# A mixture-of-experts tail on one core: the first top-16 inside the score stage, separate rings for weights and gathered rows

## The chip, the cores and the metric

The kernel runs on one core of a Trainium2 chip. The metric is the device time of one execution in microseconds (us). TensorE (PE) multiplies matrices, VectorE (DVE) and ScalarE (ACT) do elementwise work, GpSimd (POOL) does elementwise work and issues indirect transfers, and SyncE (SP) issues the other transfers. Each engine takes its instructions in the order in which the program lists them; semaphores order them across engines.

## What is computed

Two transformer blocks run over 512 tokens of 1024 features. The change touches only the last part, the `peer` layer of the second block, whose input `h` has been normalised. Cut to that:

```python
def peer(h, w_pq, sub_keys, expert_u, expert_v):          # 8 heads, 2 halves, 128 keys a half
    def one(xb):
        q = (xb @ w_pq).reshape(PEER_BLOCK, PEER_HEADS, 2, PEER_DKH)
        s = jnp.einsum('thpd,hpkd->thpk', q, sub_keys).astype(jnp.float32)
        sv, si = lax.top_k(s, PEER_TOPK)                   # the first top-16: 16 key sets
        cand = (sv[:, :, 0, :, None] + sv[:, :, 1, None, :]).reshape(PEER_BLOCK, PEER_HEADS, -1)
        cidx = (si[:, :, 0, :, None] * N_KEYS + si[:, :, 1, None, :]).reshape(PEER_BLOCK, PEER_HEADS, -1)
        best, pos = lax.top_k(cand, PEER_TOPK)             # the second top-16, for each head
        eidx = jnp.take_along_axis(cidx, pos, axis=-1)
        g = jax.nn.softmax(best, axis=-1)
        act = jax.nn.gelu(jnp.einsum('thkd,td->thk', expert_u[eidx], xb).astype(jnp.float32), approximate=False)
        return jnp.einsum('thk,thkd->td', (g * act).astype(xb.dtype), expert_v[eidx])
```

There are 128 x 128 experts, each with a row of 1024 numbers in `expert_u` and one in `expert_v`, and every token uses 8 x 16 = 128 of them.

## The kernel before, in words

A matrix product is made of three matmuls with operands that are split in a high and a low part (`mm3`, lines 124 to 126). `wload` (L109) brings in a block of weights: SP loads 512 KB into a place of the ring `raw` (L106), ACT rounds it to the high part `whi` (L117), and DVE, or POOL where the caller says so, subtracts to get the low part `wlo` (L118), which frees the place in the ring. Activations are split in the same way by `split` (L152, L153).

`peer` (L1565) has three stages.

1. **Score stage** (`scores`, L1646). For each of 16 key sets (8 heads x 2 halves) a block of `w_pq` is loaded and multiplied with `h` (24 matmuls), and `keys` (L1650) multiplies the result with that set's keys (4 matmuls, L1653), copies the 4 x 128 x 128 scores to `psc` (L1655) and stores them in DRAM as `scd` (L1656). The keys `sk` are loaded once as a whole. The `w_pq` loads have their low part on DVE.
2. **Route** (`route`, L1687). For each of four tiles t of 128 tokens: load that tile's scores from `scd` (L1693); 16 first top-16 (`top16`, L1678: two MAX8, two FIND_INDEX8, one MATCH_REPLACE8, here over 128 scores); turn the indices into `sf` (L1701); form 50 candidates for each head (L1708) and take 8 second top-16; find the chosen experts (`pick`, L1784) and the gates. For t = 0 the route ends there with a list of expert numbers, because the first 128 tokens fetch their rows. For the other 384 tokens, 32 batches of one-hot matrices (`oj` L1765, `oi` L1767, L1773) for each tile give, through 4 matmuls a batch (L1775), a dense table of gates, in which each of 128 blocks of 128 experts has one gate for each token and expert; the table goes to `stage` (L1777), and two thirds of it to DRAM (`gd`, L1782). `route` is a generator: at each `yield n, engine` the caller computes `n` blocks of `up` (L1795), with the low part of the weights on that engine. An `up` loads block i of `u` transposed (`uT`), multiplies with `h` of the 384 tokens (24 matmuls 128x384) and applies Gelu (L1802); in this stage the result goes to DRAM (`actd`). The first NPRE = 60 blocks are made here, 20 with the low part on POOL and 40 on DVE.
3. **Tail**, 128 blocks (the loop in `peer`). `mixed` (L1807) gets block i's activations, from `actd` if i < 60, else by an `up` here, multiplies them with the gates (`gt` loaded for two blocks at a time; the products go to a tile `ew`, L1822, L1824) and splits the product; `down` (L1830) loads block i of `v` and runs 18 matmuls of 128x512, which add to six accumulators. `mixed` runs AHEAD = 2 blocks ahead of `down`. For the first 128 tokens `gathered` (L1838) takes 256 rows, one for each partition at a time: 128 of `u` (product with `h`, L1856), then 128 of `v` (multiply-add into the output, L1869). POOL issues each row's indirect transfer (L1848), LAG = 2 rows ahead of their use. One row is taken per block while i < 60, and 196 over the 66 blocks from 60 to 125. In words of this text, the blocks below 60 are *early* ones and the others *mixed* ones. `wload`'s blocks and the gathered rows share the ring `raw` of RING = 6 places of 512 KB. After block 127 the results are scaled and added to the residual (L1616 to L1633).

The order on each engine is set when the program is built, by a scheduler that simulates the engines and picks among instructions whose inputs and buffers it holds to be ready; the places of rings and pools enter into it, so a change of a ring also changes the order.

Of the kernel before, what the change touches and what calls it, by code (L numbers as in the profile page):

```python
# [7 lines left out]
F32 = mybir.dt.float32  # L8
F32R = mybir.dt.float32r
I32 = mybir.dt.int32  # L10
U32 = mybir.dt.uint32
# [4 lines left out]
P = 128  # L16
D = 1024
# [10 lines left out]
class Kern:  # L28
# [1536 lines left out]
    def peer(self, h, first, residual, done):  # L1565

        nc, a = self.nc, self.a
        mod = self.mod2
        hhi, hlo = h
        with ExitStack() as c:  # L1570
            p0 = self.pool(c, "pe0")
            h0 = self.h0 = self.t(p0, [P, D], "h0")
            with ExitStack() as c1:
                qp = self.pool(c1, "pq")
                self.sk = self.t(qp, [P, 16, P], "sk")
                nc.sync.dma_start(self.sk, a["sk"])
                self.scores(qp, hhi, hlo, first, residual)
                done()
            pp = self.pool(c, "pe")
            self.stage = self.t(pp, [P, 2, P, 64], "stage")  # L1580
            with ExitStack() as c2:
                rp = self.pool(c2, "pr")
                self.iota16 = self.t(rp, [P, 16], "iota")
                nc.sync.dma_start(self.iota16, a["iota16"])
                self.iota = self.t(rp, [P, P], "iota128")
                nc.sync.dma_start(self.iota, a["iota128"])
                self.row0 = self.t(rp, [P, 16], "row0")
                nc.sync.dma_start(self.row0, a["row0"])
                jobs = self.route(rp, pp)
                pre = 0  # L1590
                for n, eng in jobs:
                    for _ in range(n):
                        if pre < self.NPRE:
                            self.up(pp, pre, hhi, hlo, eng)
                            pre += 1
            while pre < self.NPRE:
                self.up(pp, pre, hhi, hlo)
# [25 lines left out]
            for t in range(4):  # L1623
                for i in range(2):
                    s = slice(512 * i, 512 * i + 512)
# [3 lines left out]
                    else:  # L1629
                        z = self.raw()[:, :512]  # L1630
# [1 line left out]
                        (nc.vector if 2 * t + i > 4 else nc.gpsimd).tensor_add(xt[t][:, s], xt[t][:, s], z)  # L1632
                    nc.sync.dma_start(a["out"][t * P : t * P + P, s], xt[t][:, s])  # L1633

    NPRE = 60
    PROD = 5
    BOUND = (6, 14), (3, 8)
    BOUND2 = (6, 14), (8, 17)
    BOUND3 = (6, 12), (2, 8)
    RING = 6  # L1640
    AHEAD = 2
    EARLY = 2
    LAG = 2
    WB = 3

    def scores(self, p, hhi, hlo, first, residual):  # L1646

        nc, a = self.nc, self.a

        def keys(m, q):  # L1650
            pk = self.mm_ps()
            for t in range(4):
                nc.tensor.matmul(pk[:, t * P : t * P + P], q[:, t * P : t * P + P], self.sk[:, m], start=True, stop=True)  # L1653
            s = self.t(p, [P, 4, P], "psc", bufs=2)
            nc.scalar.copy(s, pk.rearrange("p (t k) -> p t k", t=4))  # L1655
            nc.sync.dma_start(a["scd"].rearrange("t p m k -> p t m k")[:, :, m], s)  # L1656

        h = list(zip(hhi, hlo))
        qs = [self.t(p, [P, S], "pq", bufs=3) for _ in first]
        self.halves(first, h, lambda n, ps, cs: nc.scalar.copy(qs[n][:, cs], ps[:, cs]), lambda i: None)  # L1660
        last = list(enumerate(qs))
        norm = self.last_hi, self.last_split
        for m in range(len(first), 16):
            with self.after(*norm):
                w = self.cut(*self.wload(a["w_pq"][m]))
            ps = self.mm_ps()
            self.proj_feat(w, h, ps)
            for z in last:
                keys(*z)
            q = self.t(p, [P, S], "pq", bufs=3)  # L1670
            nc.scalar.copy(q, ps)
            last = [(m, q)]
            if 4 <= m < 12:
                with self.after(*norm):
                    residual(m - 4)
        keys(*last[0])
# [10 lines left out]
    def route(self, p, pp):  # L1687

        nc, a = self.nc, self.a
        dve, pool = nc.vector, nc.gpsimd  # L1690
        for t in range(4):
            sc = self.t(p, [P, 16, P], "sc", bufs=1)
            nc.sync.dma_start(sc, a["scd"][t])  # L1693
            sv = self.t(p, [P, 16, 16], "sv", bufs=1)
            si = self.t(p, [P, 16, 16], "si", U32, bufs=1)
            for m in range(16):
                self.top16(p, sc[:, m], P, sv[:, m], si[:, m], "v2")
                if m % 4 == 3:
                    yield 1 + (t == 0), pool
            sf = self.t(p, [P, 16, 16], "sf", bufs=1)  # L1700
            nc.vector.tensor_copy(sf, si)  # L1701

# [11 lines left out]
            pos = self.t(p, [P, 8, 16], "pos", U32, bufs=1)  # L1714
            for h in range(8):
                self.top16(p, cand[:, h], 50, best[:, h], pos[:, h], "v3")
            yield 2, dve
            pf = self.t(p, [P, 8, 16], "pf", bufs=1)
            nc.vector.tensor_copy(pf, pos)

# [15 lines left out]
            nc.vector.tensor_sub(pf, pf, df)  # L1736
            fj = self.t(p, [P, 8, 16], "fj", bufs=1)
            self.pick(p, pf, self.iota16, f4[:, :, 1], fj, ALU.is_equal)
            yield 2, dve
            g = self.t(pp, [P, 8, 16], "gate0") if t == 0 else self.t(p, [P, 8, 16], "gate", bufs=1)  # L1740
            nc.vector.tensor_sub(g, best, best[:, :, 0:1].to_broadcast([P, 8, 16]))
            nc.scalar.activation(g, g, AF.Exp)
            s = self.t(p, [P, 8], "gs", bufs=1)
# [11 lines left out]
            tp = self.sc_ps()  # L1755
# [3 lines left out]
            for b in range(32):  # L1759
# [16 lines left out]
                st = self.stage[:, b // 16]  # L1776
                nc.scalar.copy(st[:, :, 4 * (b % 16) : 4 * (b % 16) + 4], ps.rearrange("p (t i) -> p i t", t=4))  # L1777
                if b % 4 == 3:
                    yield 1, dve
                if t < 3 and b % 16 == 15:  # L1780
                    for q in range(4):
                        nc.sync.dma_start(a["gd"][2 * (t - 1) + b // 16, :, 32 * q : 32 * q + 32], st[:, 32 * q : 32 * q + 32, :])  # L1782
# [24 lines left out]
    def mixed(self, p, i, hhi, hlo):  # L1807

        nc, a = self.nc, self.a
        if i < self.NPRE:  # L1810
            act = self.t(p, [P, 384], "act", bufs=3)
            nc.sync.dma_start(act, a["actd"][i])
        else:
            act = self.up(p, i, hhi, hlo)
        for n in ((0, 2) if i == 0 else (i + 2,)):
            if n % 2 == 0 and n < P:
                self.gates[n // 2] = self.t(p, [P, 4, 2, 64], "gt", bufs=3)
                nc.sync.dma_start(self.gates[n // 2], a["gd"].rearrange("q j i t -> j q i t")[:, :, n : n + 2])
        w = self.t(self.vp, [P, 3, P], "ew", bufs=2)
        a3 = act.rearrange("p (n t) -> p n t", n=3)  # L1820
        half = lambda z: z.rearrange("p (q t) -> p q t", t=64)
        nc.vector.tensor_mul(half(w.rearrange("p n t -> p (n t)")[:, :256]), half(act[:, :256]),  # L1822
                             self.gates[i // 2][:, :, i % 2])
        nc.vector.tensor_mul(half(w[:, 2]), half(a3[:, 2]), self.stage[:, :, i])  # L1824
        whi = self.t(self.vp, [P, 3, P], "ewh", F32R, bufs=self.AHEAD + 2)
        wlo = self.t(self.vp, [P, 3, P], "ewl", F32R, bufs=self.AHEAD + 2)
        self.split(w, whi, wlo)
        return whi, wlo
# [9 lines left out]
    def gathered(self, p, h0):  # L1838
# [4 lines left out]
        queue = []  # L1843

        def fetch(k):
            z = self.raw()
            src = a["u"] if k < P else a["v"].rearrange("i j d -> (i j) d")
            nc.gpsimd.indirect_dma_start(z, None, src, bass.IndirectOffsetOnAxis(ap=idx[:, k % P : k % P + 1], axis=0))  # L1848
            queue.append(z)
# [31 lines left out]
    def scratch(self):  # L1881
# [1 line left out]
        self.a["xs"] = dp.tile([8, P, S], F32, tag="xs", name="xs")  # L1883
        self.a["x2"] = dp.tile([4, P, D], F32, tag="x2", name="x2")
        self.a["growd"] = dp.tile([1, D], F32, tag="growd", name="growd")
        self.a["scd"] = dp.tile([4, P, 16, P], F32, tag="scd", name="scd")
        self.a["gd"] = dp.tile([4, P, P, 64], F32, tag="gd", name="gd")
        self.a["actd"] = dp.tile([self.NPRE, P, 384], F32, tag="actd", name="actd")
        self.a["rows"] = dp.tile([4, 8, P], F32, tag="rows", name="rows")
# [150 lines left out]
```

## Time and profile before

| | |
|---|---|
| runs | 3645.66 us median of 3 (3639.0 to 3648.67) |
| profiled execution, its own time | 3644.18 us |
| its span, first to last instruction | 3642.1 us |
| mean granted clock of TensorE | 0.992 of full speed |
| PE busy | 3505.6 us, 96% of the span |
| DVE busy | 2624.4 us, 72% |
| ACT busy | 1590.9 us, 44% |
| POOL busy | 774.2 us, 21% |

The time of an execution is 2.1 us more than its span. A share of busy time is a mean over stages of different kinds, so the rows below are by stage: the score stage's key sets run from 2279 to 2371 us of the span, the route from 2371 to 2758, the early blocks from 2762 to 3001, the mixed blocks from 3001 to 3633, and the output after that.

### The profile page before, as it was taken

The page shows a single profiled execution, that of the slowest core. Times are in us where ns is not written, and L with a number is a line of the kernel's source. Part 1 is how long each engine was busy: PE and PEld are TensorE (multiplying, and loading weights), DVE is VectorE, ACT ScalarE, POOL GpSimd, SP SyncE. Part 2 cuts the span into 40 slices and gives each one's busy share as a digit, 9 for nine tenths or more (in the row PEclk, how much of TensorE's full clock was granted, in tenths as well). Part 3 has the DMA queues.
Part 4 walks back from the last instruction along what each step waited for, and adds up shares of the span by engine and source line. Part 5 has one row for each costly group of instructions (what it writes and reads, how often), then busy time and mean ns, then how long its engine had stood idle before and what let it go on. Part 6 is the DMA issues. An engine that isn't in the chain of part 4 may idle for free.

```text
span 3642.1 us, 53180 instructions
## 1 busy us (share of the span) xinstructions
PE 3505.6 (96%) x19035; PEld 3036.0 (83%) x19035; DVE 2624.4 (72%) x6192; ACT 1590.9 (44%) x3137; POOL 774.2 (21%) x890
## 2 busy tenths in 40 slices
PE   6999999999999999999999999999988999999998
PEld 5899888888888987888888768889987888788787
DVE  6788677874478864488736675189998887777777
ACT  4676533413367754342334554334554333333332
POOL 4223101000232320010012212021101223333232
PEclk9999999999999999999999999999999999999999
DMA  5211266673321122446632112455556998888887
GB/s 197 70 37 56 77 202 203 219 237 103 107 70 60 53 70 70 143 147 219 204 122 65 56 39 102 140 175 165 200 180 219 336 329 290 294 308 301 294 290 267
DMA packets 228821, 611.33 MB, mean 168 GB/s; under 512 B 24070, under 2 KB 89638, under 8 KB 225868
## 3 DMA queue, kind: packets, MB, share of 16 engines
q1 hardware_dynamic: 191692, 473.69, 39.1%
q0 software_dynamic: 36864, 134.23, 11.1%
q8 instruction: 150, 2.46, 0.3%
q14 instruction: 115, 0.94, 0.1%
HBM read 566.66 MB, written 41.18 MB: 167 GB/s over the span
## 4 chain that ended last, share of the span: by engine, by line
PE 67%; DVE 13%; DMA 12%; ACT 4%; issue 3%; POOL 0%; SPq 0%; DVEq 0%; ACTq 0%; POOLq 0%
PE mm L124 16%; PE mm L125 16%; PE mm L126 16%; DMA raw<-uT 8%; DVE wlo L118 4%; DMA raw<-v 3%; ACT whi L117 3%; PE pv L552 1%; DVE oi L1773 1%; PE tr L126 1%; PE tr L124 1%; PE tr L125 1%; PE sc L496 1%; PE mm L1775 1%; DVE oj L1765 1%
## 5 line engine op out<-in xcount | busy, mean ns | idle before, releaser
L117 ACT CAST whi<-raw 128x1024 fp32r<-128x1024 f32 (+2 forms) x603 | 610.2, 1015 | 1153.5 <-PE mm L125 411.5
L118 DVE TENSOR_TENSOR wlo<-raw,whi 128x1024 fp32r<-128x1024 f32 (+2 forms) x583 | 686.8, 1180 | 445.6 <-ACT whi L117 383.6
L126 PE MATMUL tr<-hhi,wlo 128*128 128x384 f32 x1024 | 356.4, 348 | 24.1 <-DVE wlo L118 23.7
L124 PE MATMUL tr<-hhi,whi 128*128 128x384 f32 x1024 | 353.0, 345 | 18.0 <-ACT whi L117 13.6
L124 PE MATMUL mm<-hhi,whi 128*128 128x512 f32 (+1 forms) x976 | 366.6, 376 | 0.2 <-ACT mr L746 0.2
L125 PE MATMUL mm<-hlo,whi 128*128 128x512 f32 (+1 forms) x976 | 363.6, 373 | 1.8 <-DVE hlo L153 1.2
L126 PE MATMUL mm<-hhi,wlo 128*128 128x512 f32 (+1 forms) x976 | 363.2, 372 | 0.0
L125 PE MATMUL tr<-hlo,whi 128*128 128x384 f32 x1024 | 349.4, 341 | 0.0
L124 PE MATMUL mm<-whi,hhi 128*128 128x384 f32 (+2 forms) x896 | 308.6, 345 | 21.1 <-ACT hhi L152 13.7
L229 DVE CUSTOM_DVE_ANT_0 adaj<-adaw,cr 128x256 f32<-128x256 f32 x620 | 271.5, 438 | 57.4 <-DMA adaw<-ada_w 43.8
L125 PE MATMUL mm<-wlo,hhi 128*128 128x384 f32 (+2 forms) x896 | 308.4, 344 | 2.8 <-DVE wlo L118 2.8
L126 PE MATMUL mm<-whi,hlo 128*128 128x384 f32 (+2 forms) x896 | 305.9, 342 | 0.0
L282 POOL TENSOR_TENSOR nsum<-nsum,nsq 128x256 f32<-128x256 f32 x78 | 68.9, 887 | 1099.7 <-ACT nsq L280 1098.1
L1848 POOL DMA_INDIRECT raw<-u,idx x128 | 144.9, 1132 | 460.1 <-DVE act L1856 320.3
L126 PEld LDWEIGHTS tr<-hhi,wlo 128*128 128x128 f32 x1024 | 196.0, 191 | 40.9 <-DVE wlo L118 39.7
L124 PEld LDWEIGHTS tr<-hhi,whi 128*128 128x128 f32 x1024 | 196.4, 192 | 31.1 <-ACT whi L117 23.4
L125 PEld LDWEIGHTS mm<-hlo,whi 128*128 128x128 f32 x976 | 183.8, 188 | 34.0 <-DVE hlo L153 1.7
L124 PEld LDWEIGHTS mm<-hhi,whi 128*128 128x128 f32 x976 | 183.6, 188 | 33.5 <-issue 0.7
L126 PEld LDWEIGHTS mm<-hhi,wlo 128*128 128x128 f32 x976 | 183.7, 188 | 32.5 <-issue 0.3
L124 PEld LDWEIGHTS mm<-whi,hhi 128*128 128x128 f32 x896 | 171.6, 191 | 37.2 <-ACT hhi L152 13.8
L125 PE MATMUL mm<-wlo,ewh 128*128 128x512 f32 x512 | 201.4, 393 | 0.0
L126 PE MATMUL mm<-whi,ewl 128*128 128x512 f32 x512 | 199.6, 392 | 0.0
(602 smaller groups left out, 8390.1 us busy)
## 6 DMA issues: line engine op xcount, KB each, us to landing
adaw<-ada_w SPq DMA_DIRECT2D x139, 512.0 KB
raw<-uT SPq DMA_DIRECT2D x128, 512.0 KB
raw<-v SPq DMA_DIRECT2D x128, 512.0 KB
raw<-w_up SPq DMA_DIRECT2D x64, 512.0 KB
raw<-w_dn SPq DMA_DIRECT2D x64, 512.0 KB
raw<-w_b SPq DMA_DIRECT2D x48, 384.0 KB
raw<-w_aqk SPq DMA_DIRECT2D x32, 512.0 KB
raw<-w_g SPq DMA_DIRECT2D x32, 512.0 KB
```

The lines of the kernel that those rows point to most:

```text
L117: nc.scalar.copy(hi[:, :n], raw[:, :n])
L118: self.last_lo = (eng or nc.vector).tensor_sub(lo[:, :n], raw[:, :n], hi[:, :n])
L124: mm(ps, ah, bh, start=start, stop=False)
L125: mm(ps, ah, bl, start=False, stop=False)
L126: mm(ps, al, bh, start=False, stop=stop)
L229: nc.vector.tensor_tensor_reduce(junk, wt[:, q * 256 : q * 256 + 256], cond[:, q * 256 : q * 256 + 256], op0=ALU.mult, op1=ALU.add, scale= ...
L282: add_ins = (nc.vector if k == 7 else nc.gpsimd).tensor_add(tot, tot, sq)
L496: self.nc.tensor.matmul(ps, q, hi, start=True, stop=False)
L552: nc.tensor.matmul(po[:, cols], wT[:, kt], v[:, kt, hl * P : hl * P + P], start=(kt == 0), stop=(kt == 3))
L1765: nc.vector.tensor_tensor(oj, io, cb(1), ALU.is_equal)
L1773: nc.vector.tensor_scalar(oi[:, n], self.iota, one(0), one(2), ALU.is_equal, ALU.mult)
L1848: nc.gpsimd.indirect_dma_start(z, None, src, bass.IndirectOffsetOnAxis(ap=idx[:, k % P : k % P + 1], axis=0))
```

## The change

- The 64 first top-16 (16 key sets x 4 tiles) move from the route into `keys`, where they read `psc` directly; their results stay in SBUF (`self.tops`). The 16 stores to `scd` and the 4 loads from it go. The keys are loaded by set, 16 times 64 KB. The low part of 14 blocks of `w_pq` goes from DVE to POOL.
- All `up`s of the route have their low part on DVE, the points at which they are made are spread anew, and NPRE is 54.
- In the tail the ring `raw` has 4 places and holds weights only; gathered rows have a ring `row` of LAG + 1 = 4 places, with LAG = 3. The gate products are written over the activations instead of into `ew`, and the gates `gt` have 4 places instead of 3.

```diff
@@ peer
+            c2 = ExitStack()
+            tp = self.pool(c2, "pt")
+            self.tops = [(self.t(tp, [P, 16, 16], "sv", bufs=4), self.t(tp, [P, 16, 16], "si", U32, bufs=4)) for _ in range(4)]
             with ExitStack() as c1:
                 qp = self.pool(c1, "pq")
-                self.sk = self.t(qp, [P, 16, P], "sk")
-                nc.sync.dma_start(self.sk, a["sk"])
...
-                for n, eng in jobs:
+                for n in jobs:
                     for _ in range(n):
                         if pre < self.NPRE:
-                            self.up(pp, pre, hhi, hlo, eng)
+                            self.up(pp, pre, hhi, hlo)
...
-    NPRE = 60
+    NPRE = 54
...
-    RING = 6
+    RING = 4
...
-    LAG = 2
+    LAG = 3
@@ scores
         def keys(m, q):
             pk = self.mm_ps()
+            sk = self.t(p, [P, P], "sk", bufs=3)
+            nc.sync.dma_start(sk, a["sk"][:, m])
...
             nc.scalar.copy(s, pk.rearrange("p (t k) -> p t k", t=4))
-            nc.sync.dma_start(a["scd"].rearrange("t p m k -> p t m k")[:, :, m], s)
+            for t in range(4):
+                self.top16(p, s[:, t], P, *(z[:, m] for z in self.tops[t]), "v2")
...
-                w = self.cut(*self.wload(a["w_pq"][m]))
+                w = self.cut(*self.wload(a["w_pq"][m], eng=nc.gpsimd))
@@ route
-            sc = self.t(p, [P, 16, P], "sc", bufs=1)
-            nc.sync.dma_start(sc, a["scd"][t])
-            sv = self.t(p, [P, 16, 16], "sv", bufs=1)
-            si = self.t(p, [P, 16, 16], "si", U32, bufs=1)
-            for m in range(16):
-                self.top16(p, sc[:, m], P, sv[:, m], si[:, m], "v2")
-                if m % 4 == 3:
-                    yield 1 + (t == 0), pool
+            sv, si = self.tops[t]
...
-            yield 2, dve
+            yield 2 + (t == 0)
...
-            yield 2, dve
+            yield 4 - (t == 0)
...
-                    yield 1, dve
+                    yield 1 + (t == 3 and b > 8)
@@ mixed
-                self.gates[n // 2] = self.t(p, [P, 4, 2, 64], "gt", bufs=3)
+                self.gates[n // 2] = self.t(p, [P, 4, 2, 64], "gt", bufs=4)
...
-        w = self.t(self.vp, [P, 3, P], "ew", bufs=2)
-        a3 = act.rearrange("p (n t) -> p n t", n=3)
+        w = act.rearrange("p (n t) -> p n t", n=3)
         half = lambda z: z.rearrange("p (q t) -> p q t", t=64)
-        nc.vector.tensor_mul(half(w.rearrange("p n t -> p (n t)")[:, :256]), half(act[:, :256]),
-                             self.gates[i // 2][:, :, i % 2])
-        nc.vector.tensor_mul(half(w[:, 2]), half(a3[:, 2]), self.stage[:, :, i])
+        nc.vector.tensor_mul(half(act[:, :256]), half(act[:, :256]), self.gates[i // 2][:, :, i % 2])
+        nc.vector.tensor_mul(half(w[:, 2]), half(w[:, 2]), self.stage[:, :, i])
@@ gathered
         def fetch(k):
-            z = self.raw()
+            z = self.t(self.vp, [P, D], "row", bufs=self.LAG + 1)
```

**DVE at the start of the score stage.** `hlo` are the splits of the layer's input, `wlo` the low parts of `w_pq`, `psc` the scores of one key set. Before:

```order
L153 TENSOR_TENSOR hlo_22606<-nh_22355,hhi_22598 128x256
L153 TENSOR_TENSOR hlo_22608<-nh_22357,hhi_22600 128x256
L118 TENSOR_TENSOR wlo_22785<-raw_22782,whi_22784 128x1024
L118 TENSOR_TENSOR wlo_22834<-raw_22831,whi_22833 128x1024
L118 TENSOR_TENSOR wlo_22875<-raw_22872,whi_22874 128x1024
```

With the change:

```order
L153 TENSOR_TENSOR hlo_22605<-nh_22354,hhi_22597 128x256
L153 TENSOR_TENSOR hlo_22607<-nh_22356,hhi_22599 128x256
L1685 MAX sv_22632<-psc_22828 128x8
L1685 MAX sv_22634<-psc_22828 128x8
L1685 MAX sv_22636<-psc_22828 128x8
L1685 MAX sv_22638<-psc_22828 128x8
L1686 MAX_INDEX si_22633<-sv_22632,psc_22828 128x8
L1687 MATCH_REPLACE v_4697_22830<-sv_22632,psc_22828 128x128
L1685 MAX sv_22632<-psc_22861 128x8
```

The low parts of `w_pq` have left DVE, and the first top-16 stand in their place, with the four tiles of a key set, and those of the next set, interleaved. Nothing ahead of this point differs on DVE.

**PE at the end of the route.** `tr` is the bank of an `up`, 128x384; `mm` with `oi`, `oj` are the one-hot matmuls of a batch; the first row with `ewh` is the first `down`. Before, at the last `up`:

```order
L125 MATMUL tr_27615<-hlo_22609,whi_27611 128x384
L126 MATMUL tr_27615<-hhi_22601,wlo_27612 128x384
L1775 MATMUL mm_26231<-oi_26233,oj_26232 128x128 x4
L1775 MATMUL mm_26244<-oi_26246,oj_26245 128x128 x4
L1775 MATMUL mm_26291<-oi_26293,oj_26292 128x128 x4
```

With the change, first at the last `up`, then at the first `down`:

```order
L125 MATMUL tr_27419<-hlo_22608,whi_27415 128x384
L126 MATMUL tr_27419<-hhi_22600,wlo_27416 128x384
L1771 MATMUL mm_26963<-oi_26965,oj_26964 128x128 x2
L1771 MATMUL mm_26977<-oi_26979,oj_26978 128x128
...
L1771 MATMUL mm_27353<-oi_27355,oj_27354 128x128 x4
L1771 MATMUL mm_27366<-oi_27368,oj_27367 128x128 x4
L124 MATMUL mm_27452<-whi_27490,ewh_27466 128x512
```

Of 384 one-hot matmuls 168 stood behind the last `up` (42 batches of four); with the change 64 do (16 batches).

**DVE in a mixed block.** `h_4673_...` is the sum of the gathered `v` rows, `ew` or `act` the gate product. Before:

```order
L118 TENSOR_TENSOR wlo_32703<-raw_32700,whi_32702 128x1024
L153 TENSOR_TENSOR ewl_32589<-ew_32585,ewh_32588 128x384
L118 TENSOR_TENSOR wlo_32743<-raw_32740,whi_32742 128x1024
L1869 SCALAR_TENSOR_TENSOR h_4673_22629<-raw_32694,act_5614_27710,h_4673_22629 128x1024
L1869 SCALAR_TENSOR_TENSOR h_4673_22629<-raw_32697,act_5614_27710,h_4673_22629 128x1024
L1822 TENSOR_TENSOR ew_32660<-act_32656,gt_32510 128x256
```

With the change:

```order
L118 TENSOR_TENSOR wlo_32579<-raw_32576,whi_32578 128x1024
L1863 SCALAR_TENSOR_TENSOR h_4673_22628<-row_32463,act_5592_27512,h_4673_22628 128x1024
L1863 SCALAR_TENSOR_TENSOR h_4673_22628<-row_32529,act_5592_27512,h_4673_22628 128x1024
L118 TENSOR_TENSOR wlo_32684<-raw_32681,whi_32683 128x1024
L1863 SCALAR_TENSOR_TENSOR h_4673_22628<-row_32532,act_5592_27512,h_4673_22628 128x1024
L1817 TENSOR_TENSOR act_32497<-act_32497,gt_32279 128x256
```

The multiply-adds now read places named `row`, and the low part of the `uT` block `raw_32681` stands ahead of that of the `v` block `raw_32648`, which the program creates earlier: `uT` blocks are cast further ahead than before.

## Rows read from the trace of the kernel before

**Rows 1.** The page: the span, and the chain that ended last by line

```profile
span 3642.1 us, 53180 instructions
...
PE mm L124 16%; PE mm L125 16%; PE mm L126 16%; DMA raw<-uT 8%; DVE wlo L118 4%; DMA raw<-v 3%; ACT whi L117 3%; PE pv L552 1%; DVE oi L1773 1%; PE tr L126 1%; PE tr L124 1%; PE tr L125 1%; PE sc L496 1%; PE mm L1775 1%; DVE oj L1765 1%
```

**Rows 2.** By stage: us, PE PEld DVE ACT POOL busy, PEclk, DMA share, GB/s

```profile
2279.00:2371.00 92.00, 92.00 (x485) 79.11 (x483) 12.99 (x11) 33.19 (x57) 7.20 (x3) 1.00 0.50 144
2378.00:2692.00 314.00, 300.50 (x1832) 297.06 (x1833) 313.35 (x1178) 139.57 (x239) 48.53 (x20) 0.98 0.54 184
2692.00:2758.00 66.00, 50.48 (x336) 46.59 (x335) 64.78 (x177) 36.83 (x84) 0.00 (x0) 0.90 0.25 86
2762.00:3001.00 239.00, 236.88 (x1033) 194.43 (x1032) 198.84 (x350) 89.45 (x116) 59.22 (x57) 0.99 0.96 329
3001.00:3633.00 632.00, 597.92 (x2901) 523.68 (x2901) 474.71 (x615) 194.97 (x274) 210.62 (x198) 0.99 0.85 294
```

**Rows 3.** Waits among the mixed blocks, 3001 to 3633 us

```profile
ACT whi L117 <- DMA raw<-uT: 403.6, 67, 7.9
```

**Rows 4.** The chain from 3440 to 3520 us: start us, us, what

```profile
3456.04 1.23 DVE wlo L118
3457.29 6.75 DMA raw<-uT
3464.06 1.06 ACT whi L117
...
3477.45 8.25 DMA raw<-v
```

**Rows 5.** Timeline of PE: `up` matmuls after the score stage, the first `down`

```profile
2371.21 0.34 PE L124 MATMUL tr<-hhi,whi 128*128 128x384 f32 x1
...
2375.03 0.34 PE L125 MATMUL tr<-hlo,whi 128*128 128x384 f32 x1
...
2761.58 0.60 PE L124 MATMUL mm<-whi,ewh 128*128 128x512 f32 x1 [2.98 <-ACT ewh L152]
```

**Rows 6.** PE's groups from 2600 to 2691 us: busy, mean ns, idle before

```profile
L124 PE MATMUL tr<-hhi,whi 128*128 128x384 f32 x120 | 41.4, 345 | 0.0
...
L1775 PE MATMUL mm<-oi,oj 128*128 128x128 f32 x246 | 33.2, 275 | 0.0
```

**Rows 7.** Timeline of DVE at the route's start: start us, us, instruction, idle before

```profile
2378.30 1.26 DVE L1681 MAX8 sv<-sc 128x8 f32<-128x128 f32 x6 [6.37 <-DMA sc<-scd]
...
2387.01 1.76 DVE L1708 TENSOR_TENSOR cand<-sv 128x64 f32<-128x64 f32 x5
...
2399.04 0.28 DVE L1701 CAST sf<-si 128x256 f32<-128x256 uint32 x1
```

**Rows 8.** ACT's copies of the scores: shortest, median and longest in ns, first and last start

```profile
L1655 ACT COPY psc<-mm x16: 578/589/598, 2278.9 to 2370.5; 128x512 f32<-128x512 f32 x16
```

**Rows 9.** Low parts made on POOL, ns (shortest, median, longest)

```profile
L118 POOL TENSOR_TENSOR wlo<-raw,whi x20: 2339/2415/4484, 2352.8 to 2602.8; 128x1024 fp32r<-128x1024 f32 x20
```

**Rows 10.** Timeline of DVE at the end of the route

```profile
2756.95 1.11 DVE L1773 TENSOR_SCALAR oi<-iota,col 128x128 f32<-128x128 f32 x4
```

**Rows 11.** Low parts on DVE in the route: busy us, mean ns, idle before

```profile
L118 DVE TENSOR_TENSOR wlo<-raw,whi 128x1024 fp32r<-128x1024 f32 x40 | 49.6, 1241 | 0.0
```

**Rows 12.** PE's waits from 2378 to 2692 us: us in total, times, longest

```profile
PE sc L1757 <- DVE fi L1734: 4.4, 1, 4.4
PE tr L124 <- ACT act L1802: 4.3, 2, 2.4
PE tr L126 <- DVE wlo L118: 3.3, 4, 1.3
PE mm L1775 <- DVE oi L1773: 3.1, 1, 3.1
```

**Rows 13.** POOL's issues of gathered `v` rows, ns

```profile
L1848 POOL DMA_INDIRECT raw<-v,idx x125: 932/938/1871, 3213.1 to 3597.5; - x125
```

**Rows 14.** The multiply-adds on DVE among the mixed blocks: busy, mean ns, idle before

```profile
L1869 DVE SCALAR_TENSOR_TENSOR h<-raw,act,h 128x1024 f32<-128x1024 f32 x127 | 162.4, 1279 | 1.5
```

More of the change, by code (lines that the diff above doesn't have):

```diff
@@ L1572, in peer @@
             h0 = self.h0 = self.t(p0, [P, D], "h0")
+            c2 = ExitStack()
+            tp = self.pool(c2, "pt")
+            self.tops = [(self.t(tp, [P, 16, 16], "sv", bufs=4), self.t(tp, [P, 16, 16], "si", U32, bufs=4)) for _ in range(4)]
             with ExitStack() as c1:
                 qp = self.pool(c1, "pq")
-                self.sk = self.t(qp, [P, 16, P], "sk")
-                nc.sync.dma_start(self.sk, a["sk"])
                 self.scores(qp, hhi, hlo, first, residual)
                 done()
-            pp = self.pool(c, "pe")
+            pp = self.pool(c, "pe", side="right")
             self.stage = self.t(pp, [P, 2, P, 64], "stage")
-            with ExitStack() as c2:
+            with c2:
                 rp = self.pool(c2, "pr")
@@ L1651, in keys @@
             pk = self.mm_ps()
+            sk = self.t(p, [P, P], "sk", bufs=3)
+            nc.sync.dma_start(sk, a["sk"][:, m])
             for t in range(4):
-                nc.tensor.matmul(pk[:, t * P : t * P + P], q[:, t * P : t * P + P], self.sk[:, m], start=True, stop=True)
+                nc.tensor.matmul(pk[:, t * P : t * P + P], q[:, t * P : t * P + P], sk, start=True, stop=True)
             s = self.t(p, [P, 4, P], "psc", bufs=2)
             nc.scalar.copy(s, pk.rearrange("p (t k) -> p t k", t=4))
-            nc.sync.dma_start(a["scd"].rearrange("t p m k -> p t m k")[:, :, m], s)
+            for t in range(4):
+                self.top16(p, s[:, t], P, *(z[:, m] for z in self.tops[t]), "v2")
         h = list(zip(hhi, hlo))
@@ L1689, in route @@
         nc, a = self.nc, self.a
-        dve, pool = nc.vector, nc.gpsimd
         for t in range(4):
-            sc = self.t(p, [P, 16, P], "sc", bufs=1)
-            nc.sync.dma_start(sc, a["scd"][t])
-            sv = self.t(p, [P, 16, 16], "sv", bufs=1)
-            si = self.t(p, [P, 16, 16], "si", U32, bufs=1)
-            for m in range(16):
-                self.top16(p, sc[:, m], P, sv[:, m], si[:, m], "v2")
-                if m % 4 == 3:
-                    yield 1 + (t == 0), pool
+            sv, si = self.tops[t]
             sf = self.t(p, [P, 16, 16], "sf", bufs=1)
@@ L1885, in scratch @@
         self.a["growd"] = dp.tile([1, D], F32, tag="growd", name="growd")
-        self.a["scd"] = dp.tile([4, P, 16, P], F32, tag="scd", name="scd")
         self.a["gd"] = dp.tile([4, P, P, 64], F32, tag="gd", name="gd")
```

## The prediction

> **What bounds the kernel now.** I read the chain that ended last first [rows 1]: 48% of the span is the three `mm` lines of `mm3`, and `uT` transfers are 8%. That is a mean over stages, so next I read the busy times by stage (the numbers of instructions stand in brackets) [rows 2]. In the score stage PE is busy all 92.0 us, DVE only 13.0. From 2378 to 2692 DVE is full (313.4 of 314.0) and PE is not (300.5), so the route is bound by DVE. From 2692 to 2758 DVE is still full and PE has only one-hot matmuls. The early blocks are bound by PE (236.9 of 239.0). The mixed blocks are bound by PE with holes: 597.9 of 632.0.
>
> What fills the holes: ACT waits 403.6 us for `uT` blocks there, 67 times, once a block [rows 3]. The chain in a piece of that stage runs in a loop: a `uT` block lands, ACT rounds it, DVE subtracts (1.23 us), and that frees the place for the next transfer, which takes 6.75 us, another one 8.25 [rows 4]. So the shared ring of six sets the pace where it should run ahead. The transfers themselves are not at their limit: share 0.85 and 294 GB/s, against 0.96 and 329 among the early blocks [rows 2].
>
> **Prices.** PE starts an `up` matmul every (2375.03 - 2371.21) / 22 = 0.174 us [rows 5], which is 0.175 at the granted clock of 0.98 to 0.99 of the long stages; a `down` matmul takes 236.9 / 1033 = 0.23 us of PE in the early blocks [rows 2]. From 2600 to 2691 PE never idles: three groups of 120, 120 and 121 `up` matmuls are 62.8 us, which leaves 28.2 us for 246 one-hot instructions and four transposes, 0.113 us each [rows 6]. (A one-hot matmul counts as two instructions.) A first top-16 costs DVE 1.17 us: the first tile's sixteen lie between 2378.30 and 2399.04, with 1.76 us of candidate sums among them, so (20.7 - 1.8) / 16, rounded down a little for strays [rows 7].
>
> **The change part by part.**
>
> *Score stage.* Four top-16 for each key set are 4.7 us on DVE. The sets follow each other every (2370.5 - 2278.9) / 15 = 6.1 us [rows 8], and DVE loses its 14 low parts of `w_pq`, so PE covers them. `psc` has two places, and ACT's next copy waits until the four top-16 have read one: 4.7 is below 6.1. The low part on POOL takes 2.42 us, at worst 4.48 [rows 9], once a set, hidden likewise. The smaller loads of keys take no more of the queue than the stores that go. Zero, and if the cover went, the cost would be 16 times what exceeds 6.1.
>
> *Route, DVE's side.* It ends at 2758.1 now [rows 10]. Off come 48 top-16 of the other three tiles (56.2), and the first tile's: its index cast, now at 2399.04, can start at 2371.1 plus 4.7 for the last key set's top-16 plus 2.5 for two low parts, 2378.3 [rows 7, 8], which is 20.7 earlier; the 6.37 us wait for the scores from DRAM goes within that. On come nine more low parts, 49 after the first candidates against 40, at 1.24 [rows 11]: 11.2. DVE would end at 2692.4.
>
> *Route, PE's side.* At 2371.2 one `up` is done. 53 more are 1272 matmuls x 0.175 = 222.6, and 640 one-hot instructions ahead of the last `up` x 0.113 = 72.3, which gives 2666.1. Behind it are 16 batches at DVE's pace: 42 batches took the 66 us from 2692 to 2758 [rows 2], 1.57 each, so 25.1 more: 2691.2. Both sides come to the same place, so neither has slack, and PE waits for hand-offs. Now it waits 15.1 us in four places [rows 12], 20.7 with all that the floor leaves out (314 less 1392 x 0.175 less 440 x 0.113). I take 7.5 again, 4.4 for the first transposes and 3.1 for the first one-hots, which depend on the route's own order; the other two rows belong to `up`s short of weights at the start. The bounds are 0 and twice 20.7. The route ends at 2698.7, and 3.5 later the first `down` starts [rows 5, 10]: 2702.2.
>
> *Early blocks.* 1033 matmuls at 18 a block are 57.4 blocks in 239.0 us, 4.16 each [rows 2]; six fewer are 51.4 x 4.16 = 213.8, to 2916.0. Six `up`s move to the tail in exchange.
>
> *Mixed blocks.* Now 1632 x 0.175 + 1269 x 0.23 = 577.5 of 632.0: 54.5 lost, 0.80 for each of 68 `up`s. With the change there are 74 `up`s, 1776 x 0.175 = 310.8, and (2304 - 51.4 x 18) = 1379 `down` matmuls x 0.23 = 317.2, in all 628.0. How much is still lost is not in the trace, since no stage has `up`s with a ring of their own. The lower bound is zero, the upper 74 x 0.80 = 59.3. I take 5, the 0.8% that PE loses in the early blocks, because the loop that made the holes opens up: four places for two loads a block are two blocks (17 us) from one use of a place to the next, while a place needs the transfer (8.25 at the longest), rounding (1.06) and subtraction (1.23), 10.5 us [rows 4]. Rows no longer hold places: before, six places served two loads and three rows a block. In-place gate products keep an activation until its split; there are three places, DVE is busy 474.7 / 68 = 7.0 us a block, 1.6 short of 8.56, and I price it at zero; that cover gone, an `up` waits for a split of the block before, about a microsecond. So 633.0, to 3549.0, or 8.56 a block against 9.3. Transfers then need two blocks of 0.524 MB, 202/72 = 2.8 rows of the same size and 0.13 of gates, 2.65 MB a block or 310 GB/s, below the 329 that the early blocks reach.
>
> *End and sum.* 3549.0 + 9.1 after the last `down` + 2.1 around the span = **3560**, against the profiled execution's 3644.2. That stands 1.5 below the median of the runs, too little to correct for; a measurement tells about 0.3% from no change.
>
> **The rivals.**
>
> *The tail keeps its holes.* The transfers may bind rather than the ring: 0.85 is a mean, and the scheduler puts loads in another order. Then the loss is 59.3 instead of 5: **3615**. For it: the 6.75 and 8.25 us of a transfer [rows 4] show a loaded queue, and more data will move per microsecond. Against: 329 GB/s among the early blocks.
>
> *PE and DVE wait for each other in the route.* Both sides of it are full, each in program order. If PE loses the 20.7 again and DVE as much, the stage is 41.4 over its floor instead of 7.5: **3594**. For it: PE lost that while DVE was full. Against: from 2600 to 2691 PE has no idle time beside a full DVE. Both rivals together give 3649, no change.
>
> *Slower: the gathered rows' own loop.* Before, a row could take any of six places; now a place returns after four rows, and the loop of four is issue (0.94) [rows 13], landing, and multiply-add (1.28) [rows 14]. At 2.8 rows a block the loop sets the pace of the mixed blocks if it takes over 8.56 / 2.81 x 4 = 12.2 us, and the whole gain is gone at 633.0 + 83.9 = 716.9 us of mixed blocks, 9.69 each, or a landing of 11.6 us. At 12.5, half again the longest seen, (12.5 + 2.2) / 4 x 2.81 = 10.3 a block gives **3693**. Against it: 8.25 us is the longest in the piece of the chain that I read, of a plain load in the same traffic. The gathers' issue shows a spread, 932 to 1871 ns about a median of 938 [rows 13], and POOL's low parts 2339 to 4484 [rows 9], as if some other engine held them up. The Trainium skill ("SBUF — State Buffer", "Who interferes with whom") says that a DVE instruction with two SBUF inputs contends with a GpSimd instruction that reads SBUF, and that the one to issue second blocks for the whole instruction. By that rule the trace's longest issue, twice the median, agrees; were every issue that long, the loop of four would be 0.9 us longer and still below 12.2, so the sum stays, and this rival gets 3 in 100 instead of 2.
>
> **How the numbers follow.** The forecast has 0.62, the tail that keeps its holes 0.17, the route's hand-offs 0.14, both together 0.03, the slower loop 0.03; 0.01 is for ends below my low bound. Low: the route without PE's waits, at DVE's 2692.4 (6.3 less), no loss in the mixed blocks (5), early blocks at 18 x 0.23 (1), and the mixed blocks at full clock, 1% of 628 (6.3): 3541. High: 3615, the first rival, half of whose chance lies above; with both together and the slower loop about 0.15 is left out. Faster by over 0.3% (below 3633): 0.62 + 0.17 + 0.14 + 0.01 = 0.94; no change 0.03; slower 0.03.
>
> **What would show it right or wrong.** Score stage: MAX8 and FIND_INDEX8 on DVE, PE still full, end near 2371, no wait for scores from DRAM after it. Route: last one-hot matmul near 2699, DVE and PE both over 95% busy. Early blocks: 4.16 us each. Mixed blocks: 8.56 us each, the wait for `uT` no longer followed by idle PE, share of the transfers near 0.9. Wrong if PE waits for `whi` or `wlo` among the mixed blocks as often as before; if multiply-adds on DVE wait for `row`; if the key sets come further apart than 6.1 us; or if the early blocks slow down behind activations that are held longer.

## The result

The changed kernel takes **3542.32 us** (median of 4 runs, 3541.0 to 3552.44) against 3643.4 for the kernel before (4 runs, 3639.0 to 3648.67): ratio 0.9723, 95% interval 0.9707 to 0.974. The forecast was 3560 with a range of 3541 to 3615. So faster was right, by 101 us where 84 were forecast, and the time lies at the low end of the range.

The profiled execution is the 3552.44 us one. A dip of TensorE's clock at 2092 us, ahead of all that the change touches, makes it some 10 us longer (last section), so its stages are compared below from marks of their own.

### The profile after

Busy time by stage, after (us, then PE, PEld, DVE, ACT and POOL busy with the number of instructions, clock, DMA share, GB/s), as in [rows 2]: score stage, route up to its last part, the rest of the route, early blocks, mixed blocks.

```profile
2288.00:2380.60 92.60, 92.60 (x489) 79.63 (x488) 74.49 (x483) 33.71 (x58) 26.38 (x11) 1.00 0.35 111
2380.60:2676.00 295.40, 292.92 (x1901) 291.92 (x1900) 280.44 (x820) 155.89 (x280) 0.00 (x0) 0.99 0.54 188
2676.00:2703.00 27.00, 20.87 (x154) 19.21 (x152) 25.23 (x71) 15.15 (x35) 0.00 (x0) 1.00 0.11 33
2705.50:2912.80 207.30, 207.04 (x906) 171.25 (x907) 173.41 (x309) 76.61 (x105) 53.59 (x54) 0.99 0.97 343
2912.80:3541.70 628.90, 628.90 (x3172) 571.35 (x3171) 505.64 (x661) 219.70 (x299) 281.30 (x205) 1.00 0.89 312
```

PE is busy in all of the score stage although DVE now has 74.5 us of work there instead of 13.0. The mixed blocks have no holes: 628.9 of 628.9, where 34 us stood idle before [rows 2]. The chain that ended last answers to [rows 1]; PE is 93% of it now, and no transfer is left among its lines:

```profile
PE 93%; DVE 2%; ACT 2%; issue 1%; POOL 1%; DMA 1%; SPq 0%; DVEq 0%; ACTq 0%; POOLq 0%
PE mm L124 19%; PE mm L125 19%; PE mm L126 18%; PE tr L124 5%; PE tr L126 5%; PE tr L125 5%; PE mm L1771 2%; PE sc L124 2%; PE sc L125 2%; PE sc L126 2%; PE pv L552 1%; PE sc L496 1%; PE sc L497 1%; PE pv L637 1%; PE ta L548 1%
```

All waits of PE from 2370 to 3560 us (total, times, longest), the first and the last of which answer to [rows 12]; none lies in a mixed block:

```profile
PE mm L1771 <- ACT oi L1767: 4.0, 3, 1.5
PE mm L124 <- ACT ewh L152: 3.0, 1, 3.0
PE tr L124 <- ACT act L1798: 2.5, 1, 2.5
PE mm L1771 <- DVE oi L1769: 2.0, 4, 0.8
```

The marks of the stages are ACT's copies of the scores, which answer to [rows 8], and the timeline of PE at the first `down`:

```profile
L1658 ACT COPY psc<-mm x16: 578/589/602, 2288.8 to 2379.9; 128x512 f32<-128x512 f32 x16
```

```profile
2701.62 1.17 PE L1771 MATMUL mm<-oi,oj 128*128 128x128 f32 x8 [0.46 <-DVE oi L1769]
2705.76 0.50 PE L124 MATMUL mm<-whi,ewh 128*128 128x512 f32 x1 [2.98 <-ACT ewh L152]
```

| stage, us | before | forecast of the saving | after | saving |
|---|---|---|---|---|
| score stage, first to last copy | 91.6 | 0 | 91.1 | 0.5 |
| route, last copy to first `down` | 391.1 | 59.4 | 325.9 | 65.2 |
| early and mixed blocks, first `down` to the end of the last | 872.3 | 24.6 | 836.9 | 35.4 |
| together | 1355.0 | 84.0 | 1253.9 | 101.1 |

The forecast counted the tail from an end of the last `down` at 3633.0 us before, 0.9 early, so its 24.6 belongs to that mark. Six `up`s, 25 us of PE's time, moved from the route to the mixed blocks. So without them the route gave about 40 us and the tail about 60.

### The profile page after: what moved, and what is told of

Same layout as the page of the kernel before. It is cut to its first block, busy times and chain, and to the rows that moved or that the text cites. A ratio compares the mean times of both kernels' runs of the same rounds, so it can differ in the third digit from the quotient of the medians.

```text
span 3550.7 us, 53168 instructions
## 1 busy us (share of the span) xinstructions
PE 3470.9 (98%) x19035; PEld 3025.2 (85%) x19035; DVE 2614.0 (74%) x6198; ACT 1593.5 (45%) x3137; POOL 813.9 (23%) x884
## 4 chain that ended last, share of the span: by engine, by line
PE 93%; DVE 2%; ACT 2%; issue 1%; POOL 1%; DMA 1%; SPq 0%; DVEq 0%; ACTq 0%; POOLq 0%
PE mm L124 19%; PE mm L125 19%; PE mm L126 18%; PE tr L124 5%; PE tr L126 5%; PE tr L125 5%; PE mm L1771 2%; PE sc L124 2%; PE sc L125 2%; PE sc L126 2%; PE pv L552 1%; PE sc L496 1%; PE sc L497 1%; PE pv L637 1%; PE ta L548 1%
## 5 line engine op out<-in xcount | busy, mean ns | idle before, releaser
L118 DVE TENSOR_TENSOR wlo<-raw,whi 128x1024 fp32r<-128x1024 f32 (+2 forms) x589 | 694.0, 1180 | 303.0 <-ACT whi L117 298.2
L126 PE MATMUL tr<-hhi,wlo 128*128 128x384 f32 x1024 | 347.1, 339 | 0.0
L1842 POOL DMA_INDIRECT row<-u,idx x128 | 162.7, 1271 | 615.2 <-ACT stage L1773 345.4
L1842 POOL DMA_INDIRECT row<-v,idx x128 | 170.8, 1335 | 207.5 <-DVE h L1863 185.2
```

Of the source, the lines that this page charges most:

```text
L118: self.last_lo = (eng or nc.vector).tensor_sub(lo[:, :n], raw[:, :n], hi[:, :n])
L126: mm(ps, al, bh, start=False, stop=stop)
```

## The experiments

Twelve kernels. Each ran beside the kernel before on its chip, whose median was 3644 to 3650 us. "Early" is the time for a block from the first `down` to the first `up` behind it, "mixed" the time from there to the end of the last `down`; the changed kernel has 4.12 and 629.8 us.

### The two halves

**x1: the changed kernel with the old tail.**

```diff
-    RING = 4
+    RING = 6
-    LAG = 3
+    LAG = 2
-            z = self.t(self.vp, [P, D], "row", bufs=self.LAG + 1)
+            z = self.raw()
...
+        w = self.t(self.vp, [P, 3, P], "ew", bufs=2)
```

> The changed kernel with the old tail: one ring of six places for weights and rows, LAG 2, the gate product in its own tile, three places for gates. Score stage, route and the 54 blocks ahead stay as changed. If the tail's holes come from the shared ring, 0.80 us for each of 74 `up`s return: about 59 us over the changed kernel, 3601 us (3593 to 3610), and ACT waits for `uT` transfers again in every mixed block. If the tail part of the change is worth little and the gain came from the route, it stays below 3560.

3602.9 us (3593.56 to 3617.01), ratio 0.9892 [0.9861, 0.9923]. Mixed 675.6, early 4.28 a block: some 8 of the 58 us by which this tail is longer than the changed one lie in the early blocks, on which the prediction had laid nothing. What PE waits for in x1 among the mixed blocks, 2915 to 3590 us, is what it waited for in the kernel before, 3001 to 3633 us, the parts of `uT`. First x1, then before:

```profile
PE tr L126 <- DVE wlo L118: 22.1, 38, 0.7
PE tr L124 <- ACT whi L117: 9.1, 13, 1.8
```

```profile
PE tr L126 <- DVE wlo L118: 20.4, 35, 0.6
PE tr L124 <- ACT whi L117: 13.6, 17, 1.9
```

The changed kernel has neither row. DVE waits for no gathered row in x1, so in the shared ring it is the weights that come late, not the rows.

**x2: the kernel before with the new tail** (the same edit the other way).

> The kernel before with the new tail alone (weights ring of four, row ring of four, LAG 3, product in place, four gates); the first top-16 stays in the route, 60 blocks ahead. If the shared ring made the holes, the mixed blocks lose none of their 54.5 us: 3643 - 55 = 3588 us (3580 to 3595), and with x1 the two halves add up to the whole. If the parts need each other, or the tail is bound by transfers, it stays above 3615.

3587.91 us (3586.11 to 3593.59), ratio 0.9851 [0.9834, 0.9867]. PE is busy in all 581 us of its mixed blocks:

```profile
2995.00:3576.00 581.00, 581.00 (x2929) 527.64 (x2928) 477.94 (x622) 203.40 (x276) 266.04 (x199) 1.00 0.90 320
```

Against their references x1 shows 41.6 us for the score stage and route, x2 56.6 for the tail, 98 of the 101 together: the parts hardly need each other. (The change also gives the pool `pe` the argument `side="right"`; x1 has it, x2 has not, and no run tries it alone.)

### Which part of the tail

**x12: three places for weights, three for rows.** `RING = 3`, `LAG = 2`.

> The changed kernel with three places for weights and three for rows (LAG 2): six in all, as many as the shared ring had, but apart. If it is the separation that counts, three weight places are 1.5 blocks or 12.7 us between two uses of one, over the 10.5 us that a place needs, and the time stays within 3541 to 3556 us. If it is the number of places (eight against six), it is near 3601.

3570.12 us (3567.09 to 3570.97), ratio 0.9794 [0.9778, 0.981]: between the two expectations, so I took the rings one at a time.

**x4: four for weights, three for rows.** `LAG = 2`.

> The changed kernel with three places for rows (LAG 2) and four for weights. Three and three cost 28 us over four and four (3570 against 3542). If the third row place short is what cost it, this takes 3560 to 3575 us and DVE waits for `row` transfers among the mixed blocks; if it is the weights' fourth place, 3541 to 3549.

3564.66 us (3561.27 to 3572.09), ratio 0.9773 [0.9741, 0.9804]. The missing fourth place for rows is what cost it, not the weights' fourth. DVE's groups that take the rows, in x4 from 2920 to 3540 us (busy us, mean ns, idle before and its cause):

```profile
L1863 DVE SCALAR_TENSOR_TENSOR h<-row,act,h 128x1024 f32<-128x1024 f32 x126 | 161.6, 1282 | 65.4 <-DMA row<-v,idx 65.0
L1850 DVE CUSTOM_DVE_ANT_0 row<-row,h 128x1024 f32<-128x1024 f32 x74 | 88.6, 1221 | 35.1 <-DMA row<-u,idx 35.1
```

and in the changed kernel:

```profile
L1863 DVE SCALAR_TENSOR_TENSOR h<-row,act,h 128x1024 f32<-128x1024 f32 x127 | 162.5, 1280 | 3.3 <-DMA row<-v,idx 2.5
L1850 DVE CUSTOM_DVE_ANT_0 row<-row,h 128x1024 f32<-128x1024 f32 x76 | 90.0, 1221 | 15.0 <-DMA row<-u,idx 15.0
```

With three places DVE stands 100 us for rows, with four 18. PE loses 25 of the 100 (mixed 654.6). The trace shows 16 of these as waits (2903 to 3557 us), 9.8 of them for low parts of `v`, which stand behind the rows in DVE's order; where the other 9 lie it doesn't show.

```profile
PE mm L125 <- DVE wlo L118: 9.8, 10, 2.9
```

`LAG` sets the places for rows (LAG + 1) and how far ahead of its use a row is issued, so x4, x5 and x12 change both; no run says which of the two counts.

**x6: three for weights, four for rows.** `RING = 3`.

> The mirror: three places for weights, four for rows (LAG 3). If the weights' fourth place is what three and three lacked, 3560 to 3575 us, with ACT waiting for `uT` transfers and PE behind it; if it is the rows', 3541 to 3549.

3543.41 us (3537.44 to 3547.91), ratio 0.9713 [0.9682, 0.9744]: as fast as the change, so with four places for rows the fourth weight place is worth nothing. Its waits among the mixed blocks hold a lesson; first x6, then the changed kernel:

```profile
ACT whi L117 <- DMA raw<-uT: 264.6, 69, 6.5
```

```profile
ACT whi L117 <- DMA raw<-uT: 6.3, 3, 3.9
```

ACT waits 265 us for `uT`, in the changed kernel 6.3, and mixed is 629.8 us in both. This is the kind of row on which my prediction laid the holes [rows 3]. An idle ACT that waits for the next block says that ACT is early, not that PE is short of weights.

**x5: two places for rows.** `LAG = 1`.

> The changed kernel with two places for rows (LAG 1), weights with four. It prices the rival in which the rows' own loop sets the pace: issue, landing and multiply-add of one row, with two places, pass for two rows. With 1.1 us for the issue, 5 to 7 for the landing and 1.28 for the multiply-add a block of 2.81 rows takes 10.4 to 13.2 us instead of 8.5, and the time is 3680 to 3890 us, slower than the kernel before. If rows wait for nothing but their turn on DVE, three places would have cost nothing, and two cost as little: under 3600.

3670.94 us (3667.75 to 3688.87), ratio 1.0081 [1.0048, 1.0113]: slower than the kernel before, but less than expected. Mixed is 741.8 us for 74 `up`s, 10.0 a block. If the rows' loop sets that, two rows take 10.0 x 2 / 2.81 = 7.1 us, of which 7.1 - 1.2 - 1.28 = 4.7 is left for the landing, an estimate; I had put 5 to 7. (1.2 is the median issue of a `v` row in the changed kernel, where [rows 13] had 0.94.) By the same loop three places take 6.7 us a block, below 8.5, and should have cost nothing, which x4 contradicts. The likely reason, not tested, is that a mean over a block does not cover rows that DVE takes two or three in a row.

### The product in place

**x13: rows and weights in one ring of six, all else as changed.**

```diff
-    RING = 4
+    RING = 6
-    LAG = 3
+    LAG = 2
-            z = self.t(self.vp, [P, D], "row", bufs=self.LAG + 1)
+            z = self.raw()
```

> The changed kernel with rows and weights in one ring of six and LAG 2; the gate product stays in place and the gates keep four places. If the ring is the cause, it is as slow as x1, 3601 us (3593 to 3610). If the product in place or the fourth place of the gates does it, it stays below 3556.

3630.94 us (3628.03 to 3638.58), ratio 0.9964 [0.9952, 0.9976]: a miss. It is 28 us slower than x1, from which it differs by the product in place and a fourth place for gates (not tried apart), and the difference lies in the early blocks, 4.81 us each against 4.28, 27 us in all. In them (2704 to 2951 us) DVE waits for activations from DRAM, 2.5 us of it in x1, and PE for low parts of `v` behind it on DVE:

```profile
DVE act L1817 <- DMA act<-actd: 68.3, 34, 4.7
PE mm L125 <- DVE wlo L118: 22.8, 20, 2.5
```

**x14 and x15: four and two places for activations** instead of x13's three, each the one edit `bufs=3` to `bufs=4` or `bufs=2` where `act` is made.

> x13 with a fourth place for activations. x13 (shared ring, product in place) took 28 us more than x1 (shared ring, product in its own tile), and 27 of them in the early blocks, where SP waits 53.7 us for a split before it may load the next activation into one of three places, with the loads of `v` behind it. If the activations that are held longer are the cause, this comes back to x1: 3603 us (3595 to 3612), early blocks near 4.3 us. If it is the order of the rows or the gates, it stays at 3631.

> x13 with two places for activations instead of three, the other way from x14. If a lack of places had made x13's early blocks slow, this is slower still, over 3640 us. If the order is the cause (with three places DVE's gate product for block 35, with four that for 36, stands next to the low part of `v` block 30, while SP loads activations only three to five blocks ahead of `v`), two places bring the product back to block 32, DVE stops waiting for activations from DRAM, and the early blocks take 4.1 to 4.4 us instead of 4.8: 3603 us (3595 to 3612), faster with a place less.

x14 took 3642.93 us (3635.04 to 3653.18), ratio 0.9995 [0.9981, 1.001], slower than either branch of its expectation, x15 3615.78 us (3611.58 to 3619.43), ratio 0.9922 [0.9899, 0.9944].

| | places | DVE's product beside the low part of `v` block 30 | early, us a block | DVE's wait for `actd` there, us |
|---|---|---|---|---|
| x15 | 2 | block 32 | 4.48 | 57.8 |
| x13 | 3 | block 35 | 4.81 | 68.3 |
| x14 | 4 | block 36 | 5.02 | 79.4 |

More places make it slower. With each the scheduler moves the product, which must wait for a load from DRAM, further ahead of the low part of `v`, on which PE waits; both are on DVE, in order. So places were not short, and the order changed with them. But the order on DVE is not the whole cause: x1 and the kernel before have block 35 in that place too, and DVE waits 2.5 and 1.6 us there, and the changed kernel has block 32, as x15 has, and waits 6.8. In x1 SP issues the load of an activation five blocks ahead of the `v` block, in x13 three: an activation that is overwritten in place keeps its place until its split. How far ahead the load comes seems to count as much as the order, and no run separates them. x15's expectation was right in sign and half right in size (3603 was expected): the waits are shorter, not gone.

### The route and the blocks ahead

**x8: 42 blocks ahead.** `NPRE = 42`.

> The changed kernel with 42 blocks ahead instead of 54: the last twelve `up`s of the route are not made there but in the tail. DVE saves 12 x 1.24 = 14.9 us in the route, PE 12 x 4.2 = 50.4, all of which it does later. If DVE sets the route's end as soon as PE has less work, the route ends 14.9 us earlier, PE idles 35.5 us more, and the time is 3578 us (3570 to 3586). If PE's side sets it, the work only moves and the time stays at 3542.

3574.14 us (3572.94 to 3581.03), ratio 0.9796 [0.9768, 0.9824], 32 us more, as expected within 4. That is in part luck: the route ends 25 us earlier, not 15, so DVE had more slack at 54 than I gave it, and by my own sum 50.4 - 25 = 25 us were due. The profiled executions, which both have the dip of the last section, differ by 28.6 us: the tail grows by 53.5, where I had 50.4. Behind its last `up`, by stage as above, DVE is full (81.1 of 83.0 us) and PE is not:

```profile
2595.00:2678.00 83.00, 63.27 (x439) 57.70 (x437) 81.11 (x227) 47.36 (x109) 0.00 (x0) 0.94 0.34 122
```

**x11: 60 blocks ahead**, the six more in the last half of the third tile.

```diff
-    NPRE = 54
+    NPRE = 60
-                    yield 1 + (t == 3 and b > 8)
+                    yield 1 + (t >= 2 and b > 8)
```

> The changed kernel with 60 blocks ahead, the six more `up`s in the last half of the third tile's one-hots. DVE does 7.4 us more in the route; PE moves 25.2 us of work there and can fill the 6 us in which it waits behind the last `up`. If both sides of the route are in balance at 54, the time is within 6 us of the changed kernel, 3538 to 3548. If DVE sets the route's end, it is 7 us later and the time 3549.

3599.94 us (3595.03 to 3602.54), ratio 0.987 [0.9845, 0.9896]: a miss, and not chiefly in the route. That takes 351.0 us instead of 325.9. The 25.1 more look like the six `up`s, but are not: PE's own work there ends 16.5 us later (339.4 us behind the last score copy, against 322.9), as it fills its waits, and the first `down` then waits 11.7 us for its split, not 3.0. The loss is in the early blocks, 5.08 us each. Their order is that of x13, the product for block 35 beside the low part of `v` block 30, and DVE waits 83.9 us for activations there. PE's wait ahead of the first `down`, and DVE's in the early blocks (2722 to 3006 us):

```profile
PE mm L124 <- ACT ewh L152: 11.7, 1, 11.7
```

```profile
DVE act L1817 <- DMA act<-actd: 83.9, 37, 4.3
```

x2, which has the same tail and also 60 blocks ahead, has block 34 in that place, waits 14.4 us and takes 4.12 us a block. So 60 blocks need not cost this. That the order around them does is likely, but not tested, and as in x13 it is not the order alone.

**x9: the low parts of `w_pq` on DVE again**, without `eng=nc.gpsimd` in `scores`.

> The changed kernel with the low parts of `w_pq` on DVE again, next to the top-16. By durations DVE has 4.7 + 1.24 = 5.9 us of work for each key set against PE's 6.1, so the score stage stays covered: 3541 to 3549 us, sets 6.1 us apart. If a low part that stands behind a top-16 which waits for its scores holds up PE, the sets come 7 us or more apart and the time is over 3556.

3542.05 us (3540.68 to 3553.79), ratio 0.972 [0.9688, 0.9753], sets 6.10 us apart: no difference. DVE is busy 85.1 of 91.0 us of the score stage, and PE all of it:

```profile
2277.00:2368.00 91.00, 91.00 (x482) 78.62 (x481) 85.06 (x488) 32.25 (x56) 0.00 (x0) 1.00 0.36 111
```

That part of the change wasn't needed.

No kernel beats the changed one beyond the noise. Between the first score copy and the last `down` its PE stands idle only some 8 us in the route and 3 before the first `down`.

## Why the prediction was right, point by point

- *Score stage at zero.* Right. Sets are 6.07 us apart against 6.1, with 74.5 us of DVE's work in 92.6 us, 4.9 a set; x9 shows 5.7 (85.1 in 91.0) still covered.
- *Route, PE's side, 2691.2.* Right. Its last one-hot group ends at 2702.8 in a profile in which the score stage ends 9.4 us later, so at 2693.4, 2.2 behind the floor: 4.4 late at the end of the last `up` (2679.9, so 2670.5 against 2666.1), and 2.2 made up behind it, where the 16 batches take 22.9 us instead of 25.1.
- *Route, DVE's side, 2692.4, and 7.5 us for two full engines.* This is the term that failed. DVE idles 16.7 of 322 us in the route now, 9.1 of them for PE:

```profile
2381.00:2703.00 322.00, 313.39 (x2051) 310.72 (x2049) 305.27 (x889) 170.74 (x314) 0.00 (x0) 0.99 0.51 175
```

```profile
DVE oj L1761 <- PE mm L1771: 9.1, 13, 1.5
```

  I had taken all of DVE's durations as they stood. Eleven instructions among them had stood beside POOL's low parts and taken 1.1 to 2.1 us more than the median of their kind, 18.9 us in all. Before, in the route, the products of `pick` by shortest, median and longest (ns), and two of those held up (start us, us):

```profile
L1792 DVE TENSOR_TENSOR eq<-eq,d x8: 1211/1230/2926, 2425.6 to 2663.5; 128x1024 f32<-128x1024 f32 x8
```

```profile
2425.60 2.81 DVE L1792 TENSOR_TENSOR eq<-eq,d 128x1024 f32<-128x1024 f32 x1
...
2428.60 2.20 DVE L1746 TENSOR_TENSOR gate<-gate,gs 128x128 f32<-128x128 f32 x1
```

  POOL ran two low parts meanwhile:

```profile
2424.08 6.57 POOL L118 TENSOR_TENSOR wlo<-raw,whi 128x1024 fp32r<-128x1024 f32 x2 [5.32 <-ACT whi L117]
```

  After, where POOL has nothing in the route:

```profile
L1788 DVE TENSOR_TENSOR eq<-eq,d x8: 1217/1218/1224, 2403.9 to 2559.8; 128x1024 f32<-128x1024 f32 x8
```

  I had quoted the rule for this, for the gathers alone: the Trainium skill ("SBUF — State Buffer", "Who interferes with whom") has the second of a DVE instruction with two SBUF inputs and a GpSimd one that reads SBUF blocked for the whole instruction. The trace agrees: 2.81 us for 1.22, 2.20 for 0.29. Seven of the eleven have two inputs; the other four are `TENSOR_SCALAR`, of which the rule as I quote it says nothing. So taking 20 low parts off POOL should be a gain for DVE of its own; no run moves them without the top-16. Ten of the eleven, 17.8 us, stand behind the index cast from which my sum counts, and without them DVE's side comes to 2692.4 - 17.8 = 2674.6, an estimate, clear of PE's. So the two sides were not in balance, and the route ends 2.2 us behind PE's floor, not 7.5. That the wrong term cost the forecast so little is luck: PE's side, which was right, sets the end. With 42 blocks ahead, where DVE sets it, the same error was 10 us (x8).
- *Early blocks, 4.16 us.* 4.12, with a DMA share of 0.97.
- *Mixed blocks lose 5 of 59 us.* They lose none that the trace shows (PE has no wait there, neither for `whi` nor for `wlo`), and PE's clock is 1.00 in them instead of 0.99, which is 2.5 us of `up` matmuls. Together with the early blocks this is the 10.8 us of the second half by which the forecast was long. That the shared ring made the holes was right (x1, x2), why it did only in part: x6 shows that the weights' loop needed three places, not four, and that ACT's long wait for `uT`, on which I laid the holes, can stand with no hole; x4 shows that the rows' fourth place (with its row of lead) is worth 22 us, and I had said nothing of it but that rows "no longer hold places".
- *The product in place at zero, an `up` later by a microsecond if its cover went.* Zero in the mixed blocks of the changed kernel, where PE waits for no split. The last of my signs, early blocks that slow down behind activations that are held longer, came in x13 and not here, and larger than a microsecond: 27 us in all, with the fourth place for gates not told apart from it.
- *The rivals.* "The tail keeps its holes" is out: PE has none, at a DMA share of 0.89 and 312 GB/s, above the 294 of before. "PE and DVE wait for each other" is out: the route ends 2.2 us over its floor, not 41.4. The slower loop of the rows exists, but at two places (x5), not at four.

## What to carry to other kernels

Count an engine's durations without what another engine did to them: an instruction whose longest time is many times its median was held up, what ran beside it shows by whom, and moving that other work away can be a gain. A wait row of an engine off the chain (ACT's 265 us in x6) is no loss; ask which wait ends in PE. Where a scheduler sets the order, a place more can make a kernel slower, so compare the order of the two or three instructions that matter, and how far ahead their loads come, before you blame the buffer; and try one more place for gathered rows than the mean over a block asks for.

## What the runs showed of the hardware

The granted clock dipped in a stage that no kernel here changes. The stretches 2080 to 2092, 2092 to 2100, 2100 to 2108 and 2108 to 2118 us by stage, in the profiled execution of the changed kernel:

```profile
2080.00:2092.00 12.00, 8.22 (x54) 5.26 (x54) 11.22 (x35) 8.17 (x36) 7.61 (x12) 1.00 0.14 42
2092.00:2100.00 8.00, 7.92 (x15) 3.52 (x16) 3.35 (x13) 2.14 (x8) 0.00 (x0) 0.50 0.01 4
2100.00:2108.00 8.00, 7.54 (x33) 4.72 (x32) 4.77 (x21) 4.91 (x20) 0.00 (x0) 0.50 0.00 0
2108.00:2118.00 10.00, 10.00 (x31) 6.26 (x32) 4.87 (x15) 2.18 (x8) 1.02 (x1) 0.61 0.00 0
```

and in that of the kernel before:

```profile
2080.00:2092.00 12.00, 9.96 (x59) 6.79 (x58) 10.29 (x35) 8.21 (x35) 8.90 (x15) 0.86 0.14 52
2092.00:2100.00 8.00, 6.16 (x28) 3.32 (x28) 6.57 (x28) 4.73 (x17) 0.00 (x0) 1.00 0.15 33
2100.00:2108.00 8.00, 8.00 (x47) 4.96 (x47) 6.14 (x19) 5.44 (x24) 1.88 (x1) 1.00 0.00 0
2108.00:2118.00 10.00, 9.92 (x58) 7.09 (x56) 5.91 (x19) 5.57 (x21) 3.74 (x8) 1.00 0.12 29
```

PE runs at 1.2 GHz instead of 2.4 for 24 us, after 12 us (2080 to 2092) in which it was busy 8.2 at full clock, and its first score copy comes 9.9 us later than in the kernel before (2288.8 against 2278.9). Of the 14 profiles of this case four (the changed kernel, x5, x8, x13) have their first score copy at 2287 to 2289 us, ten at 2277 to 2280. Nine of these ten have a short dip instead, as the kernel before has it (0.86 in 2080 to 2092): 3 to 7 us at 1.2 GHz that begin between 2080 and 2084, after which no delay like it shows. x4 has neither, and the four with the long dip lack the short one. What sets either off stays open. It means that one profiled execution can stand 10 us off another of the same program, and that stages are best compared from a mark of their own.
